# Both halves of a weight load split in one ACT and one DVE instruction, and the order of loads and block products that goes with it

## The chip, the cores and the metric

The kernel runs on one core of a Trainium2 chip. The metric is the device time of one execution in microseconds (us). Engines: PE multiplies matrices (PEld is its weight load), DVE, ACT and POOL work on vectors, SP issues most of the DMAs.

## The reference, cut to what matters

A two-layer encoder over 256 tokens of width 1024, in float32:

```python
for layer in range(DEPTH):                                   # DEPTH = 2
    h = h + _token_mixer(_rmsnorm(h, norm1[layer]), ...)
    h = h + _conv_ffn(_rmsnorm(h, norm2[layer]), ...)
return _rmsnorm(h, norm_f)

def _token_mixer(xn, w_in, w_pool, pool_scale, w_a, w_b, w_o, rel_bias):
    u, q, k, v, g_pool, g_attn = jnp.split(xn @ w_in, SPLITS, axis=-1)
    ...   # centred means of u; dilated attention of q, k, v with bias from rel_bias
    merged = jax.nn.sigmoid(g_pool) * (pool_out @ w_a) + jax.nn.sigmoid(g_attn) * (attn_out @ w_b)
    return merged @ w_o

def _conv_ffn(xn, w_up, conv_w, conv_b, w_down):             # d_ff = 2816
    a, gval = jnp.split(xn @ w_up, 2, axis=-1)
    a = conv of width 3 along the tokens, a channel at a time, + conv_b
    return (jax.nn.gelu(a) * gval) @ w_down
```

The weights (186 MB read from HBM) are used once each, so the kernel is a long stream: load a piece of weights, prepare it, multiply.

## The kernel before, in words

**Loads and splits.** Weights come in loads of 1 MB, `raw` in the profile (128 partitions x 4 x 512 floats; for `w_down` and `w_o` 2 x 1024). Three such buffers exist. PE multiplies in a reduced float32 form (fp32r), so each load is split in two halves of 128x1024, and each half in two terms: ACT makes `wh`, the rounded weights (a CAST, L259), and DVE makes `wl`, what the rounding lost (a subtraction, L261). There are five buffers of 128x1024 for `wh` and five for `wl`. PE then takes three products for each slice of weights: wh with x's high term, wl with it, wh with x's low term. These are the lines L798 (projections by tokens), L715, L716 and L717 (products into the residual: `w_down`, `w_o`) and L917 (block products). A 1 MB load gives 24 matmuls of 128x512.

**The class `Weights`** keeps the list of pieces (halves) in the order of their use. `_split` makes splits ahead of the products as buffers allow, and after each one calls `load(ahead(i))`, which issues loads on SP's queue. SP also issues the copies by which tensors change their layout through DRAM ("crossings": a write at L857, four reads into `zga`, `zg` and others at L864), and SP's queue runs in order. `run_between` runs steps of other work between the ACT and the DVE part of a split.

**The block.** One 2x2 block of `w_up`'s column groups in each layer's MLP (group `("w", 3)`), and one part of the projections in layer 1, are multiplied with seven products in place of eight. Each product has a name and two halves: 11, 22 and 21 take weights as loaded; T1 to T4 take sums of quadrants that DVE makes in place in a `raw` buffer (L344). 50 and 51 are the numbers of the two loads that hold these sums. In this text "T4" is the last product. The constant `BLOCK` gives the order; `"d"` stands for one piece (half a load) of `w_down`, multiplied at L715 to L717 in between. The products collect in four PSUM banks:

```python
BANK_OF = {"11": "p", "T1": "t", "22": "t", "T2": "q", "21": "p", "T3": "q", "T4": "q"}
```

T2, T3 and T4 add up in bank q. After T2 and again after T3 `add` reads bank q (a DVE sum into `kept`, L1692) and sends the result off (a DVE transpose, L852, and a crossing). So T4's matmuls can begin only when T3's `add` has read the bank. The MLP's own order is written by hand (`manual_schedule`, MLP_GROUPS, PAIR_PLACES); within a queue nothing overtakes. A half of 21, T1 to T4 or 11 is six matmuls, a "d" twelve.

**Norms.** Between the parts of a layer an RMSNorm turns the residual `h` (L607) into `xn` (L618), which PE transposes (L627); ACT and DVE make its two terms (L630, L631). During the MLP's first norm DVE also makes splits for the first groups.

**Attention bias.** `build_bias` makes the position bias of four heads and reads it from DRAM into `bt` with five DMAs (L559) once, in layer 0.

Of the kernel before, what the change touches and what calls it, by code (L numbers as in the profile page):

```python
# [52 lines left out]
    ("11", 0), ("11", 1), "d", ("T1", 0), ("T1", 1), "d", "d", ("22", 0), ("22", 1), "d", ("T2", 0), ("T2", 1), "d",  # L53
    ("21", 0), ("21", 1), "d", ("T3", 0), ("T3", 1), "d", "d", ("T4", 0), ("T4", 1),
# [64 lines left out]
class Weights:  # L119
# [6 lines left out]
    RAW, BUFS, LOOK = 3, 5, 3  # L126

    def __init__(self, tc, pool, idle, small):
# [7 lines left out]
        self.between = []  # L136
# [3 lines left out]
        self.sums = {}  # L140

    def add(self, src, shape, cuts, tag=None):

        n = len(self.loads)
        self.loads.append((src, shape, tag))
        return [(n, cut, c_shape) for cut, c_shape in cuts]

    def use(self, pieces, slots=()):
        slots = list(slots) + [None] * len(pieces)
        self.pieces += [p + (slot,) for p, slot in zip(pieces, slots)]  # L150

    def ahead(self, i):


        upto = min(n for n, *_ in self.pieces[i : i + 3])
# [52 lines left out]
    def _split(self, upto):  # L208
        nc = self.nc
        first = self.n_split  # L210
        while self.n_split < len(self.pieces):
            i = self.n_split
            n, cut, shape, slot = self.pieces[i]
            if i >= upto and (slot is None or i >= max(upto, first + 2) or i >= upto + 4 or i < 4):
                break
            if slot is None and len(self.live) == self.BUFS:
                break
            self.load(n + 1)
            with ExitStack() as queued:
                for insts, some in self.later:  # L220
                    for inst in insts if i in some else ():
# [10 lines left out]
    def run_between(self):  # L232

        while self.between:
            self.between.pop(0)()

    def open_next(self):
# [3 lines left out]
        n, cut, shape, slot = self.pieces[i]  # L241
        if slot is None:
            self.live.add(i)
            h, l = (
                self.pool.tile([P, *shape], F32R, tag=tag, bufs=self.BUFS, name=f"{tag}{i}")
                for tag in ("wh", "wl")
            )
# [44 lines left out]
    def free(self, i):  # L292
        self.live.discard(i)


@with_exitstack
def encoder(ctx, tc, x, w_in, w_pool, pool_scale, w_a, w_b, w_o, norm1, norm2, w_up, conv_w,
# [32 lines left out]
    def use_block(units, made, first):  # L330
# [9 lines left out]
        def sum_later(i, name, j):  # L340

            def make():
                one, other = terms[name]
                nc.vector.tensor_sub(out=raw(name, j), in0=raw(one, j), in1=raw(other, j))  # L344
# [3 lines left out]
        for j in range(2):  # L348
            sum_later(len(W.pieces) + first + j, "T1", j)
        behind = [u for u in units if len(u) > 2]  # L350
        for unit in units:
            if len(unit) > 2:
                W.use([unit])
                behind = behind[1:] or behind
                continue
            name, j = unit
            if name in SUMS:
                sum_later(len(W.pieces), SUMS[name], j)
            if name in ("22", "21"):
                W.use([made[name][j]])  # L360
            else:
                W.use([(behind[0][0], lambda t, name=name, j=j: raw(name, j), (2, 512))])
# [6 lines left out]
    def block(w, down, n, made):  # L369
# [3 lines left out]
        d += rows(down, 4 * P)  # L373
        made["21"] = quadrant(w, 1, DFF + n * 512)
        d += rows(down, 6 * P)
# [151 lines left out]
    bt = const.tile([P, HPG, NT * P], F32, name="bt")  # L527

    def build_bias():
# [25 lines left out]
        nc.sync.dma_start(out=fd[0].rearrange("(h e) -> h e", h=HPG), in_=fsb)  # L555
        yield
        for blk, kind in enumerate((4, 3, 1, 0, 2)):
            src = bass.AP(fd.tensor, fd.offset + kind * 256, [[1, P], [NT * 256, HPG], [1, P]])
            nc.sync.dma_start(out=bt[:, :, blk * P : (blk + 1) * P], in_=src)  # L559
        yield  # L560

    def bias_of(t, hh):

        b = bt[:, hh]
# [556 lines left out]
    for l in range(DEPTH):  # L1121
# [203 lines left out]
        if l == 0:  # L1325
            visits["u", 1, 0] = visits["u", 1, 2] = ((next, bias),)

# [439 lines left out]
```

## Time and profile before

| | before |
|---|---|
| three runs | 848.07, 847.58, 847.60 us; median 847.6 |
| profiled execution | 848.11 us, its span 846.3 us (1.8 us lie around it) |
| granted PE clock | 0.999 |
| busy | PE 838.7, PEld 699.3, DVE 665.5, ACT 531.1, POOL 35.5 us |
| moved by DMA | 214 MB, mean 253 GB/s |

Busy time of an engine that others wait for counts; busy time beside a busier engine does not. In the chain of waits each row is a piece of the work that ended last: its start, its length, the engine and the line. In the groups a row gives how often an instruction ran, its busy time and the mean of one. In the timeline the idle time before an instruction, and what ended it, stand in brackets. An instruction that starts while the one before it drains overlaps with it on paper: DVE instructions follow one another at some 0.08 us less than the length that is shown.

### The profile page before, as it was taken

What the parts mean: (1) busy time and instruction counts of PE and PEld (TensorE: products, weight loads), DVE (VectorE), ACT (ScalarE), POOL (GpSimd) and SP (SyncE); (2) the same over time, 40 slices, a digit from 0 to 9 for tenths busy, and PEclk for the clock granted to TensorE, in tenths of its full rate; (3) what the DMA queues carried; (4) which work ended last, traced back from release to release, by engine and by line L of the source; (5) the groups of instructions that cost most, each with busy time, mean ns of one, the idle gap of its engine ahead of it and who ended that gap; (6) DMA issues with size and microseconds to landing.
All of it is one profiled execution on the core that took longest, in us unless ns stands there. A gap on an engine that the chain in (4) does not pass through costs nothing.

```text
span 846.3 us, 10959 instructions
## 1 busy us (share of the span) xinstructions
PE 838.7 (99%) x3889; PEld 699.3 (83%) x3889; DVE 665.5 (79%) x860; ACT 531.1 (63%) x770; POOL 35.5 (4%) x96
## 2 busy tenths in 40 slices
PE   9999999999999999999999999999999999999997
PEld 7888888888888887888888888888888888888886
DVE  6968877757767799788898997868577867998884
ACT  7744556655554776488765555577455647757883
POOL 1720000000010000000000000000000100000000
PEclk9999999999999999999999999999999999999999
DMA  8699987796759886889857669968777499768861
GB/s 305 211 304 289 317 282 251 246 282 218 233 206 302 276 275 199 256 264 316 272 185 225 222 225 316 284 235 261 247 261 269 164 308 309 227 224 275 303 218 50
DMA packets 147967, 214.02 MB, mean 253 GB/s; under 512 B 7801, under 2 KB 69185, under 8 KB 147913
## 3 DMA queue, kind: packets, MB, share of 16 engines
q1 hardware_dynamic: 147480, 212.67, 76.8%
q10 hardware_dynamic: 432, 0.66, 0.2%
q8 instruction: 30, 0.49, 0.2%
q14 instruction: 25, 0.20, 0.1%
HBM read 186.02 MB, written 27.28 MB: 252 GB/s over the span
## 4 chain that ended last, share of the span: by engine, by line
PE 90%; DMA 3%; DVE 3%; ACT 2%; issue 1%; POOL 0%; ACTq 0%; SPq 0%; DVEq 0%; POOLq 0%
PE t_ps L798 54%; PE res_ps L716 6%; PE res_ps L715 6%; PE res_ps L717 6%; PE t_ps L917 4%; PE v_ps L798 3%; DMA raw<-in_w_up_dram 3%; PE v_ps L1101 3%; PE v_ps L917 2%; PE pool_ps L702 1%; PE v_ps L1000 1%; PE o_ps L1392 1%; PE s_ps L1344 1%; ACT wh L259 1%; DVE wl L261 1%; PE s_ps L1339 1%
## 5 line engine op out<-in xcount | busy, mean ns | idle before, releaser
L261 DVE TENSOR_TENSOR wl<-raw,wh 128x1024 fp32r<-128x1024 f32 x292 | 350.9, 1219 | 92.4 <-ACT wh L259 91.7
L798 PE MATMUL t_ps<-wh,x 128*128 128x512 f32 x1280 | 401.8, 390 | 0.0
L259 ACT CAST wh<-raw 128x1024 fp32r<-128x1024 f32 x292 | 302.1, 1048 | 158.8 <-PE t_ps L798 71.2
L798 PEld LDWEIGHTS t_ps<-wh,x 128*128 128x128 f32 x1280 | 240.3, 188 | 50.0
L798 PE MATMUL t_ps<-wl,x 128*128 128x512 f32 x640 | 249.0, 389 | 0.0
L798 PEld LDWEIGHTS t_ps<-wl,x 128*128 128x128 f32 x640 | 120.2, 188 | 24.7
L715 PE MATMUL res_ps<-wh,actq 128*128 128x512 f32 (+1 forms) x184 | 70.0, 380 | 0.0
L716 PE MATMUL res_ps<-wl,actq 128*128 128x512 f32 (+1 forms) x184 | 69.8, 380 | 0.0
L717 PE MATMUL res_ps<-wh,actk 128*128 128x512 f32 (+1 forms) x184 | 69.3, 380 | 0.0
L798 PE MATMUL t_ps<-wh,po 128*128 128x512 f32 x128 | 41.4, 395 | 0.0
L715 PEld LDWEIGHTS res_ps<-wh,actq 128*128 128x128 f32 x184 | 34.6, 188 | 6.7
L716 PEld LDWEIGHTS res_ps<-wl,actq 128*128 128x128 f32 x184 | 34.6, 188 | 6.7
L717 PEld LDWEIGHTS res_ps<-wh,actk 128*128 128x128 f32 x184 | 34.6, 188 | 6.5
L1604 ACT ACTIVATE a<-zga,prm 128x256 f32<-128x256 f32 x80 | 38.9, 512 | 0.0
L592 POOL TENSOR_SCALAR ss<-ss 128x1 f32<-128x1 f32 x8 | 3.1, 386 | 764.2 <-ACT junk L585 764.2
L344 DVE TENSOR_TENSOR raw<-raw,raw 128x1024 f32<-128x1024 f32 x24 | 29.3, 1222 | 0.0
L798 PEld LDWEIGHTS t_ps<-wh,po 128*128 128x128 f32 x128 | 24.0, 188 | 4.9
L715 PE MATMUL res_ps<-wh,m 128*128 128x512 f32 (+1 forms) x72 | 26.5, 368 | 0.0
L716 PE MATMUL res_ps<-wl,m 128*128 128x512 f32 (+1 forms) x72 | 26.3, 365 | 0.0
L717 PE MATMUL res_ps<-wh,m 128*128 128x512 f32 (+1 forms) x72 | 26.0, 365 | 0.0
L1608 DVE TENSOR_TENSOR y<-y,a 128x510 f32<-128x510 f32 x22 | 14.9, 679 | 13.6 <-ACT y L1602 13.6
L798 PE MATMUL t_ps<-wl,po 128*128 128x512 f32 x64 | 24.9, 390 | 0.0
(221 smaller groups left out, 1069.6 us busy)
## 6 DMA issues: line engine op xcount, KB each, us to landing
raw<-in_w_in_dram SPq DMA_DIRECT2D x58, 1024.0 KB
raw<-in_w_up_dram SPq DMA_DIRECT2D x40, 1024.0 KB
raw<-in_w_down_dram SPq DMA_DIRECT2D x22, 1024.0 KB
crossing<-crossing SPq DMA_DIRECT2D x22, 512.0 KB
crossing<-way SPq DMA_DIRECT2D x16, 512.0 KB
raw<-in_w_a_dram SPq DMA_DIRECT2D x8, 1024.0 KB
raw<-in_w_o_dram SPq DMA_DIRECT2D x8, 1024.0 KB
zga<-crossing SPq DMA_DIRECT2D x40, 128.0 KB
```

The source lines that it names most:

```text
L259: inst = nc.scalar.copy(out=h, in_=src)
L261: inst = self.rests[i] = nc.vector.tensor_sub(out=l, in0=src, in1=h.bitcast(F32))
L344: nc.vector.tensor_sub(out=raw(name, j), in0=raw(one, j), in1=raw(other, j))
L702: nc.tensor.matmul(out, w(k), x, start=(steps is first and k == 0), stop=(steps is last and k == nk - 1), skip_group_check=turns["rest"],)
L715: nc.tensor.matmul(ps, ah, wh, start=first, stop=False, skip_group_check=on)
L716: nc.tensor.matmul(ps, ah, wl, start=False, stop=False, skip_group_check=on)
L717: nc.tensor.matmul(ps, al, wh, start=False, stop=last, skip_group_check=on)
L798: nc.tensor.matmul(ps, x2[:, 2 * n + j, part, t, :], w[:, j, :], start=(n + m == 0), stop=(n == last and m == 5),)
L917: nc.tensor.matmul(ps, operands[name](part, 2 * j + c), w[:, c, :], start=(name in ("11", "T1") and j + m == 0), stop=(j == 1 and m == 5), ...
L1101: nc.tensor.matmul(ps[t], a[:, k, t, :], w[:, j, :], start=(k + m == 0), stop=(k == KD - 1 and m == 2),)
L1604: nc.scalar.mul(out=out, in_=a, mul=row(j, c))
L1608: nc.vector.tensor_add(out=y[:, :, 1:], in0=y[:, :, 1:], in1=t["a0"][:, :, : S - 1])
```

## The change

1. **Pairs.** Where `W.two` is set (the six projection groups with n other than 1 or of kind "u"; in the MLP all but the last two groups), both halves of a load are split by one ACT instruction and one DVE instruction of 128x2048 (L311 and L312 of the new kernel), once two neighbouring slots are free. The five `wh` and five `wl` buffers become six slots each. The sums for T1 to T4 are made over 128x2048 as well (L424).
2. **Loads.** There, `ahead` counts the `raw` buffers held, and issues the next load when one of three is given back.
3. **Orders.** `BLOCK` and `VALUES` put both halves of each unit together and change the places of the "d" pieces. Copies by ACT of the block's banks run before a split's ACT part (`at_once`) in place of after it.
4. **Bias.** `bt` holds two heads at a time. Five DMAs load the first two (SP's queue, in both layers), five more on ACT's queue the other two, in attention step 4.

```diff
 BLOCK = (
-    ("11", 0), ("11", 1), "d", ("T1", 0), ("T1", 1), "d", "d", ("22", 0), ("22", 1), "d", ("T2", 0), ("T2", 1), "d",
-    ("21", 0), ("21", 1), "d", ("T3", 0), ("T3", 1), "d", "d", ("T4", 0), ("T4", 1),
+    ("11", 0), ("11", 1), "d", "d", ("T1", 0), ("T1", 1), "d", "d", ("22", 0), ("22", 1), "d", "d",
+    ("T2", 0), ("T2", 1), "d", "d", ("T3", 0), ("T3", 1), ("21", 0), ("21", 1), ("T4", 0), ("T4", 1),
 )
...
-    RAW, BUFS, LOOK = 3, 5, 3
+    RAW, SLOTS, LOOK = 3, 6, 3
...
     def ahead(self, i):
+        if self.two:
+            upto = end = self.n_loaded
+            held = sum(
+                tag is None and self.last_use[n] > i
+                for n, (_, _, tag) in enumerate(self.loads[:upto]) if n > upto - 10
+            )
+            while held < self.RAW and end < len(self.loads) and self.not_before.get(end, i) <= i:
+                end += 1
+                if self.loads[end - 1][2] is None:
+                    held += 1
+                    upto = end
+            return upto
...
+            count = 1
+            if self.makes_two(i):
+                if self.two_slots() is not None:
+                    count = 2
+                elif i >= self.n_got + 2:
+                    break
...
-                for hi, lo, *_ in self.open_next():
+                for hi, lo, *_ in self.open_next(count):
+                    self.run_at_once()
                     hi()
                     self.run_between()
                     lo()
-                if i in self.sums:
-                    self.sums.pop(i)()
-            self.load(self.ahead(i))
+                for j in range(i, i + count):
+                    if j in self.sums:
+                        self.sums.pop(j)()
+            self.load(self.ahead(i + count - 1))
...
+                def both(n):
+                    if n == 0:
+                        return nc.scalar.copy(out=h, in_=src)
+                    inst = nc.vector.tensor_sub(out=l, in0=src, in1=h.bitcast(F32))
+                    self.rests[i] = self.rests[i + 1] = inst
+                    return inst
...
-    bt = const.tile([P, HPG, NT * P], F32, name="bt")
+    bt = const.tile([P, 2, NT * P], F32, name="bt")
...
-            4: ((W.bring_back,), (scores, 1)),
+            4: ((W.bring_back,), (scores, 1), (load_bias, 2, nc.scalar)),
...
             for kind, n in GROUPS:
+                W.two = n != 1 or kind == "u"
```

**Place 1: DVE at the end of layer 0's block.** The rows are splits (`wl<-raw,wh`), sums (`raw<-raw,raw`), `add` and its transpose. Before, raw_2535 holds T3, raw_2537 T4, raw_3004 the weights of 21, raw_2940 and raw_3006 pieces of `w_down`, raw_3087 the group after the block:

```order
290 L344 TENSOR_TENSOR raw_2537<-raw_3004,raw_2537 128x1024
291 L261 TENSOR_TENSOR wl_3060<-raw_3004,wh_3059 128x1024
292 L344 TENSOR_TENSOR raw_2537<-raw_3004,raw_2537 128x1024
293 L261 TENSOR_TENSOR wl_3071<-raw_2940,wh_3070 128x1024
294 L1692 TENSOR_TENSOR kept<-t_ps,kept 128x512
295 L852 STREAM_TRANSPOSE crossing<-kept 128x4x4x32
296 L261 TENSOR_TENSOR wl_3081<-raw_2535,wh_3080 128x1024
297 L261 TENSOR_TENSOR wl_3106<-raw_2535,wh_3105 128x1024
298 L261 TENSOR_TENSOR wl_3116<-raw_3006,wh_3115 128x1024
299 L261 TENSOR_TENSOR wl_3126<-raw_3006,wh_3125 128x1024
300 L261 TENSOR_TENSOR wl_3142<-raw_2537,wh_3141 128x1024
302 L1692 TENSOR_TENSOR kept<-t_ps,kept 128x512
```

Now raw_2311 holds T3, raw_2313 T2 and then T4, raw_2723 the weights of 21, raw_2690 two pieces of `w_down`, raw_2742 the group after the block:

```order
243 L312 TENSOR_TENSOR wl<-raw_2690,wh 128x2048
244 L312 TENSOR_TENSOR wl<-raw_2311,wh 128x2048
245 L1786 TENSOR_TENSOR kept<-t_ps,kept 128x512
246 L940 STREAM_TRANSPOSE crossing<-kept 128x4x4x32
247 L312 TENSOR_TENSOR wl<-raw_2723,wh 128x2048
248 L424 TENSOR_TENSOR raw_2313<-raw_2723,raw_2313 128x2048
249 L312 TENSOR_TENSOR wl<-raw_2313,wh 128x2048
250 L1786 TENSOR_TENSOR kept<-t_ps,kept 128x512
251 L940 STREAM_TRANSPOSE crossing<-kept 128x4x4x32
252 L312 TENSOR_TENSOR wl<-raw_2742,wh 128x2048
```

The sum that makes T4's weights stood ahead of T3's splits, with two pieces of `w_down` split after them; now it stands behind T3's and 21's splits, directly ahead of its own.

**Place 2: SP's queue at the start of layer 0's MLP.** Before (raw rows are 1 MB loads of `w_up`, crossing rows the write and zga and zg rows the four reads of a crossing):

```order
98 L178 DMA raw_2444<-in_w_up_dram 128x4x512
99 L857 DMA crossing<-crossing 128x2x512
100 L178 DMA raw_2537<-in_w_up_dram 128x4x512
101 L864 DMA zga<-crossing 32x8x128 x4
102 L178 DMA raw_2466<-in_w_up_dram 128x4x512
103 L178 DMA raw_2500<-in_w_up_dram 128x4x512
104 L857 DMA crossing<-crossing 128x2x512
105 L178 DMA raw_2539<-in_w_up_dram 128x4x512
106 L864 DMA zg<-crossing 32x8x128 x4
107 L178 DMA raw_2573<-in_w_up_dram 128x4x512
```

And now, where raw_2263, raw_2267, raw_2283, raw_2315, raw_2344 are the loads that raw_2444, raw_2466, raw_2500, raw_2539 and raw_2573 were, and raw_2313 is what raw_2537 was:

```order
98 L199 DMA raw_2263<-in_w_up_dram 128x4x512
99 L945 DMA crossing<-crossing 128x2x512
100 L199 DMA raw_2267<-in_w_up_dram 128x4x512
101 L952 DMA zga<-crossing 32x8x128 x4
102 L199 DMA raw_2283<-in_w_up_dram 128x4x512
103 L199 DMA raw_2313<-in_w_up_dram 128x4x512
104 L199 DMA raw_2315<-in_w_up_dram 128x4x512
105 L945 DMA crossing<-crossing 128x2x512
106 L199 DMA raw_2344<-in_w_up_dram 128x4x512
107 L952 DMA zg<-crossing 32x8x128 x4
```

The load that stood behind the four `zga` reads (raw_2466) now stands ahead of them, and so does raw_2573 ahead of the `zg` reads.

**Place 3: DVE in the norm ahead of layer 0's MLP.** Before (x_2207 is the second term of the transposed `xn`):

```order
216 L631 TENSOR_TENSOR x_2207<-xt_ps,x_2207 128x4x128
217 L261 TENSOR_TENSOR wl_2330<-raw_2137,wh_2329 128x1024
218 L618 SCALAR_TENSOR_TENSOR xn<-h,rstd,gain 128x256 x4
219 L631 TENSOR_TENSOR x_2207<-xt_ps,x_2207 128x4x128 x2
220 L852 STREAM_TRANSPOSE crossing<-v_ps 128x4x4x32
221 L261 TENSOR_TENSOR wl_2431<-raw_2218,wh_2430 128x1024
```

Now:

```order
189 L719 TENSOR_TENSOR x_2036<-xt_ps,x_2036 128x4x128
190 L335 TENSOR_TENSOR wl<-raw_1972,wh 128x1024
191 L335 TENSOR_TENSOR wl<-raw_2047,wh 128x1024
192 L706 SCALAR_TENSOR_TENSOR xn<-h,rstd,gain 128x256 x4
193 L719 TENSOR_TENSOR x_2036<-xt_ps,x_2036 128x4x128 x2
194 L940 STREAM_TRANSPOSE crossing<-v_ps 128x4x4x32
```

One more split of 128x1024 stands ahead of the second token half's four `xn`.

More of the change, by code (lines that the diff above doesn't have):

```diff
@@ L140, in __init__ @@
         self.sums = {}
+        self.slots = [pool.tile([P, self.SLOTS, 1024], F32R, tag=tag, name=tag) for tag in ("wh", "wl")]
+        self.freed = {slot: slot - self.SLOTS for slot in range(self.SLOTS)}
+        self.slot_of, self.n_freed = {}, 0
     def add(self, src, shape, cuts, tag=None):
@@ L338, in raw, with whole, sum_later @@
             return W.raw[made[name][0][0]][:, 2 * j : 2 * j + 2]
-        def sum_later(i, name, j):
+        def whole(name):
+            return W.raw[made[name][0][0]]
+        def sum_later(i, name):
             def make():
                 one, other = terms[name]
-                nc.vector.tensor_sub(out=raw(name, j), in0=raw(one, j), in1=raw(other, j))
+                nc.vector.tensor_sub(out=whole(name), in0=whole(one), in1=whole(other))
             W.sums[i] = make
-        for j in range(2):
-            sum_later(len(W.pieces) + first + j, "T1", j)
-        behind = [u for u in units if len(u) > 2]
+        sum_later(len(W.pieces) + first + 1, "T1")
         for unit in units:
@@ L361, in use_block @@
             else:
-                W.use([(behind[0][0], lambda t, name=name, j=j: raw(name, j), (2, 512))])
+                W.use([(
+                    made[name][0][0], lambda t, name=name, j=j: raw(name, j), (2, 512),
+                    False if j else lambda t, name=name: whole(name),
+                )])
     def first_quadrants(w, n):
@@ L1640, in at_place @@
         def at_place(p, make, *first):
+            W.at_once = [step for step in first if step in by_scalar]
+            first = [step for step in first if step not in by_scalar]
             W.between = [*first, *(step for _, _, step in sorted(between.pop(p, ()), key=lambda x: x[:2]))]
@@ L1708, in encoder @@
             for kind, n in MLP_GROUPS[1:]:
+                W.two = (kind, n) not in MLP_GROUPS[-2:]
                 ps = None
```

93 lines of the change are left out of this document (69 added, 24 removed), and 10 rows, old and new, of the table VALUES.

## The prediction

> **What bounds the kernel now.** I read the engines' busy time first, then the windows by stage (columns: length, then busy us and count of PE, PEld, DVE, ACT and POOL, the granted clock, the DMA share, GB/s), then the chain of waits where PE was not full.
>
> ```profile
> span 846.3 us, 10959 instructions
> PE 838.7 (99%) x3889; PEld 699.3 (83%) x3889; DVE 665.5 (79%) x860; ACT 531.1 (63%) x770; POOL 35.5 (4%) x96
> ```
> ```profile
> 0.00:20.00 20.00, 19.15 (x87) 15.77 (x88) 12.25 (x21) 13.66 (x26) 3.89 (x12) 1.00 0.91 321
> 20.00:240.00 220.00, 220.00 (x1035) 184.16 (x1034) 164.32 (x234) 124.58 (x174) 19.79 (x59) 1.00 0.82 267
> ...
> 300.00:320.00 20.00, 19.59 (x87) 15.81 (x86) 18.28 (x23) 16.66 (x27) 0.00 (x0) 1.00 0.78 239
> 320.00:340.00 20.00, 20.00 (x90) 16.57 (x89) 19.97 (x19) 12.54 (x14) 0.00 (x0) 1.00 0.64 210
> ...
> 420.00:440.00 20.00, 19.69 (x104) 16.19 (x103) 17.44 (x28) 12.73 (x24) 3.34 (x7) 1.00 0.70 236
> 440.00:650.00 210.00, 210.00 (x989) 176.07 (x988) 167.10 (x221) 123.86 (x165) 0.00 (x0) 1.00 0.76 245
> ```
>
> PE is the bound almost everywhere: through 220 us and again through 210 us it is never idle, although DVE and ACT work there at 75 to 80% and 57 to 59%. Making DVE and ACT cheaper is therefore worth nothing by itself. Idle PE is seen at 300 to 320 (0.41 us) and 420 to 440 (0.31 us). In 320 to 340 DVE is full (19.97 of 20) while PE still keeps going: the block lives on the distance that its splits have.
>
> The chain of waits shows PE's pace and the two stalls:
>
> ```profile
> 317.26 0.64 DVE crossing L852
> 318.03 3.03 PE t_ps L917 x12
> ...
> 337.38 2.72 PE t_ps L917 x12
> ...
> 350.98 2.72 PE t_ps L917 x12
> 353.70 32.64 PE t_ps L798 x144
> ...
> 422.87 0.50 DVE xn L618
> ...
> 429.56 0.50 DVE xn L618
> 430.10 0.83 PE xt_ps L627 x4
> ...
> 432.33 0.44 PE xt_ps L627 x4
> ```
>
> Twelve matmuls take 2.72 us and 144 take 32.64: 0.2267 us each both times, so the pace does not change with the work around it. At 318 a dozen took 3.03, 0.31 too long, which with the idle 0.41 makes a stall of 0.72. At 430 four transposes took 0.83 against 0.44, 0.39 too long, with the idle 0.31 together 0.70. No more than about 1.4 us of stalls can be won after the start, 0.17%. What a run can tell from no change is 0.2%, 1.7 us (845.9 or less; 849.3 or more).
>
> **The change, part by part.** PE does the same matmuls, so the sum is the stalls that go against the stalls that come.
>
> *Price of a pair.* No 128x2048 instruction was run. From the groups:
>
> ```profile
> L261 DVE TENSOR_TENSOR wl<-raw,wh 128x1024 fp32r<-128x1024 f32 x292 | 350.9, 1219 | 92.4 <-ACT wh L259 91.7
> L259 ACT CAST wh<-raw 128x1024 fp32r<-128x1024 f32 x292 | 302.1, 1048 | 158.8 <-PE t_ps L798 71.2 <-DMA raw<-in_w_up_dram 40.4 <-PE res_ps L717 23.5
> L1625 DVE TENSOR_TENSOR actk<-g,actq 128x512 fp32r<-128x512 f32 x22 | 15.1, 686 | 0.0
> L1624 ACT CAST actq<-g 128x512 fp32r<-128x512 f32 x22 | 13.6, 619 | 8.8 <-DVE g L1616 8.8
> ```
>
> DVE: 1219 + 2 x (1219 - 686) = 2285 ns, ACT: 1048 + 2 x (1048 - 619) = 1906 ns. Upper ends are two halves, 2.44 and 2.10. In place of two halves that saves some 0.15 and 0.19 us, on engines that do not bound. I take 2.29 and 1.91. [...]
>
> *The stall at 317 goes.* It began with a late load. SP's queue (before, place 2) held a load behind the four `zga` reads:
>
> ```profile
> 265.21 1.81 SPq L864 DMA_DIRECT2D zga<-crossing  x4
> 267.13 0.94 SPq L178 DMA_DIRECT2D raw<-in_w_up_dram  x2
> ```
> ```profile
> ACT wh L259 <- DMA raw<-in_w_up_dram: 40.4, 15, 7.5
> ```
>
> The load went out at 267.13; ACT waited up to 7.5 us for such loads, DVE fell behind and was full up to the transpose at 317.26. Now this load stands ahead of the reads and is issued when a buffer is given back, and DVE has some 0.1 us less for each pair. I take the whole 0.72 away (other end: 0, if DVE is late all the same).
>
> *The norms.* Ahead of the MLP (place 3) one more split stands ahead of the second `xn` group:
>
> ```profile
> 247.35 1.22 DVE L261 TENSOR_TENSOR wl<-raw,wh 128x1024 fp32r<-128x1024 f32 x1
> 249.02 1.67 DVE L618 SCALAR_TENSOR_TENSOR xn<-h,rstd,gain 128x256 f32<-128x256 f32 x4 [0.46 <-POOL rstd L597]
> ```
> ```profile
> 249.89 0.60 PE L627 MATMUL xt_ps<-ident,xn 128*128 128x128 f32 x4
> ```
>
> DVE was free at 248.48 (247.35 + 1.13) and waited for POOL; a further split ends that pitch at 249.61, 0.6 later than 249.02. PE's transposes started 0.05 after two `xn` were there (249.02 + 2 x 0.41). PE now does one matmul of 0.23 ahead of them, so 0.6 - 0.05 - 0.23 = 0.3 us is new idle time, in each layer: +0.6 (ends 0 and 1.2). In the norm between the layers, PE's order puts two matmuls (0.45) ahead of the second transposes, but one more split stands there too; of the 0.70 I take half away, -0.35 (ends 0 and -0.70).
>
> *The end of the block.* This is the largest term. T4's weights are now a sum that needs 21's split, which stands behind T3's split, and `add` of T3 stands behind T4's split (place 1). The block and what follows end where they did, so on PE's clock of before T2 runs from 337.38, two pieces of `w_down` from 340.10, T3 from 345.54, 21 from 348.26, T4 from 350.98, five by 2.72 us after 337.38. There are three pairs of slots: T3's split can begin only when the pieces ahead of T2 are multiplied, at 337.38. The rows for the steps:
>
> ```profile
> 324.05 1.22 DVE L261 TENSOR_TENSOR wl<-raw,wh 128x1024 fp32r<-128x1024 f32 x1
> 325.19 1.22 DVE L344 TENSOR_TENSOR raw<-raw,raw 128x1024 f32<-128x1024 f32 x1
> ...
> 338.80 0.69 DVE L1692 TENSOR_TENSOR kept<-t_ps,kept 128x512 f32<-128x512 f32 x1
> 339.53 0.71 DVE L852 STREAM_TRANSPOSE crossing<-kept 128x512 f32<-128x512 f32 x1
> 340.17 6.86 DVE L261 TENSOR_TENSOR wl<-raw,wh 128x1024 fp32r<-128x1024 f32 x6
> ```
> ```profile
> 337.42 1.06 ACT L259 CAST wh<-raw 128x1024 fp32r<-128x1024 f32 x1 [1.37 <-PE res_ps L717]
> ```
>
> A cast starts 0.04 after PE's release (337.42). Then: T3's cast to 339.33; T3's subtraction 339.40 to 341.69 (the next can start 0.08 before that); `add` of T2 at 341.61 (to the next 0.73); its transpose at 342.34 (0.64); 21's subtraction at 342.98 (2.20 to the next); the sum for T4 at 345.18 to 347.47, a subtraction priced as a split, as the two kinds are equal in the rows (1.22); T4's cast 347.50 to 349.41; T4's subtraction 349.48 to 351.77; `add` of T3 351.69 to 352.38. T4 starts at 352.45 against 350.98: a stall of 1.5 us. Before, the sums for T4 stood ahead of the `add` at 338.80 and T4's splits in the run of six at 340.17, so nothing waited. Layer 1 has the same order on both engines:
>
> ```profile
> 733.81 2.87 PE t_ps L917 x12
> ...
> 753.03 2.72 PE t_ps L917 x12
> ...
> 766.63 2.72 PE t_ps L917 x12
> ```
>
> The last two lie where 337.38 and 350.98 lie in layer 0, 415.65 later, so again 1.5: together +3.0. Ends: +4.0 if a pair costs two halves (five steps by some 0.1 more each) and the group after it is late too; +1.6 if T3's split has a slot 0.7 earlier than I read. The next group's split (raw_2742) ends about 2.2 us after `add`, at 354.6, ahead of its use at 355.2.
>
> *Elsewhere nothing.* The sums among layer 1's projections have 8 to 11 us between a slot's release and its use, one of 5.4 against a need of 4.4 (a cast, a split and their waits). (A release is a slot's last matmul; between it and the use lie 36 to 48 matmuls, once 24.) Five bias DMAs on ACT's queue stand behind the second scores' `p`, and the third scores' sums need them:
>
> ```profile
> 0.72 0.39 ACTq L475 DMA_DIRECT2D h<-in_x_dram  x1
> ```
> ```profile
> 154.33 1.32 ACT L1368 ACTIVATE p<-p,rz 128x512 f32<-128x512 f32 x2
> ```
> ```profile
> 160.64 0.68 DVE L1351 CUSTOM_DVE_ANT_0 s<-s_ps,bt 128x512 f32<-128x512 f32 x1
> ```
>
> 5 x 0.39 = 2.0 us of issue from 155.6 on; the casts behind them start 2 us later, on an ACT that is idle 41% of 440 to 650, and the last bias goes out at 157.6, 3 us before its use. Should it land late, DVE waits 1 to 2 us with its splits behind it; at 75 to 80% busy it catches up. I take 0; without that cover it would be 2 us in each layer. Start and end keep their order.
>
> **Sum.** -0.72 - 0.35 + 0.6 + 3.0 = +2.5 us. The profiled execution took 848.11 (span 846.3 and 1.8 around it), giving 850.6; it stands 0.5 above the median of the three, 847.6, so the forecast is 850.1.
>
> **The rivals.**
>
> *A, the block's end is covered: not slower.* The one mechanism is T4's chain: 13.6 us of PE from 337.38 to 350.98 against 15.1 of chain. It carries four DVE pairs and two casts. It decides at 1.5 us: if the pairs took 1.91 in place of 2.29, or T3's split began at 335.9, no stall would come. The slope of 512 to 1024 speaks against the first, the three slot pairs against the second. It would give 847.6 - 0.72 - 0.35 + 0.6 = 847.1; with half of the stall left, 848.6: both within 0.2%.
>
> *B, more of the block is late.* DVE was full at 320 to 340, and a pair's split is usable only when all of it is done, 1.1 us later than the first half was. If the first products (11, T1, 22) also meet late pairs, the stall of 317 stays (+0.7) and comes in layer 1 too (there its dozen took 2.87, 0.15 long already), and T4's end is +4.0: 847.6 + 4.0 + 0.7 + 0.6 - 0.35 = 852.6. For it speaks the full DVE, against it that loads come earlier.
>
> [...]
>
> **How the numbers follow.** Forecast (849.3 to 851.5): 0.46. A: 0.32, of which within 0.2% nearly all. B (851.5 to 853): 0.14. C: 0.08, half of it below 845.9. Slower: 0.46 + 0.14 = 0.60; faster: 0.04; within 0.2%: 0.36. The range reaches from A's low part, 846.8, to B, 852.2; outside it lie half of B and most of C. If it is slower, 849.3 to 852.
>
> **What would show it.** Right: after about 350 and 766 us PE idles 1 to 2 us ahead of a block product (L1005), released by DVE's `add` (L1786); that row stands in the waits and DVE's splits (L312) at 2.2 to 2.3 us; PE is full at 310 to 320; 0.3 idle at about 250 and 666. Wrong: PE full through both blocks' ends, L312 well under 2.2 us, or T4's cast (L311) starting at or before 346. PE idle among the projections would mean that loads or slots, which I price at nothing, run short.

## The result, and the profile after

The changed kernel takes 856.77 us (median of four runs, 854.14 to 857.12) against 847.82 (847.58 to 848.07) for the kernel before: ratio 1.0099 [1.0078, 1.0119], 9 us slower. The profiled execution is the one of 857.12.

The head of the page after, with ACT's DMA queue (q10) and, in the last three rows, the groups of the pairs (L312, L311) and of the sums (L424):

```profile
span 855.3 us, 10716 instructions
PE 841.8 (98%) x3889; PEld 699.9 (82%) x3889; DVE 657.3 (77%) x753; ACT 516.3 (60%) x675; POOL 33.8 (4%) x96
...
q10 hardware_dynamic: 3152, 1.97, 0.9%
...
L312 DVE TENSOR_TENSOR wl<-raw,wh 128x2048 fp32r<-128x2048 f32 x95 | 216.9, 2285 | 54.6 <-ACT wh L311 54.5
...
L311 ACT CAST wh<-raw 128x2048 fp32r<-128x2048 f32 x95 | 181.0, 1909 | 91.7 <-PE t_ps L886 46.7
...
L424 DVE TENSOR_TENSOR raw<-raw,raw 128x2048 f32<-128x2048 f32 x12 | 27.4, 2284 | 0.0
```

The pairs cost what was estimated (2285 ns, 1909 ns). The bias DMAs on ACT's queue show in q10, where the kernel before had 432 packets. DVE has 8.2 us less to do and ACT 14.8, and the kernel is 9 us longer. PE's waits after (line, what it waited for, us in total, times, longest) and its windows (columns as above):

```profile
PE t_ps L1005 <- DVE kept L1786: 3.1, 2, 1.5
PE xt_ps L715 <- DVE xn L706: 1.4, 2, 1.1
...
PE t_ps L886 <- DVE way L940: 0.4, 1, 0.4
PE o_ps L1478 <- DVE ptl L1469: 0.3, 1, 0.3
PE v_ps L886 <- DVE x L719: 0.3, 1, 0.3
```
```profile
0.00:20.00 20.00, 18.54 (x81) 15.36 (x82) 10.70 (x19) 12.05 (x24) 2.87 (x11) 1.00 0.90 321
...
240.00:260.00 20.00, 19.67 (x106) 16.37 (x105) 14.62 (x25) 13.10 (x23) 3.06 (x7) 1.00 0.48 164
300.00:320.00 20.00, 20.00 (x90) 16.56 (x89) 16.42 (x17) 13.91 (x20) 0.00 (x0) 1.00 0.77 258
...
340.00:360.00 20.00, 18.46 (x82) 15.00 (x81) 16.41 (x11) 11.05 (x6) 0.00 (x0) 1.00 0.43 136
420.00:440.00 20.00, 18.92 (x102) 15.68 (x100) 16.19 (x24) 13.26 (x23) 3.95 (x7) 1.00 0.88 313
580.00:620.00 40.00, 39.42 (x213) 33.62 (x213) 28.46 (x42) 24.09 (x37) 0.00 (x0) 1.00 0.87 269
```

300 to 320 is full, which it was not before; 340 to 360 has lost 1.5 us, and the wait at L1005 stands twice, once in each layer. The other losses are small and spread over places most of which the prediction had priced at nothing.

To add them up I took, from the trace, the start-to-start time of each matmul beyond its pace (0.227 us at 512 columns, 0.118 at 256, 0.111 at 128). The sum over the kernel is 8.9 us more after than before; the two spans differ by 9.0, so nothing large is missing. The rows below hold 8.4 of it; the rest lies in pieces of less than 0.2 us. Of the changed kernel there are three more profiled executions (the runs e5, e13 and e14 below), of the kernel before one more (e15):

| us lost on PE | before, two profiles | after, first | after, the other three |
|---|---|---|---|
| first 41 us | 3.4, 3.6 | 4.9 | 3.6, 4.3, 5.2 |
| layout copies near 135 | 0, 0 | 0.7 | 0, 0, 0 |
| attention, layer 0 and 1 | 0, 0 | 0.3 + 1.1 | 1.6, 1.1, 0.9 |
| norm ahead of the MLP, layer 0 and 1 | 0, 0 | 0.6 + 0.1 | 0.6, 1.5, 1.2 |
| near 317 | 0.65, 0 | 0 | 0, 0, 0 |
| T4, both layers | 0, 0 | 1.7 + 1.7 | 3.4, 3.4, 3.4 |
| between the layers | 0.75, 0.75 | 2.1 | 1.7, 1.7, 2.0 |

**T4.** DVE, then T3's cast on ACT and T4's first matmul on PE, at the end of the block after (timeline):

```profile
342.16 2.29 DVE L312 TENSOR_TENSOR wl<-raw,wh 128x2048 fp32r<-128x2048 f32 x1 [1.47 <-ACT wh L311]
344.37 0.68 DVE L1786 TENSOR_TENSOR kept<-t_ps,kept 128x512 f32<-128x512 f32 x1
...
345.72 2.25 DVE L312 TENSOR_TENSOR wl<-raw,wh 128x2048 fp32r<-128x2048 f32 x1
347.89 2.28 DVE L424 TENSOR_TENSOR raw<-raw,raw 128x2048 f32<-128x2048 f32 x1
352.23 2.29 DVE L312 TENSOR_TENSOR wl<-raw,wh 128x2048 fp32r<-128x2048 f32 x1 [2.05 <-ACT wh L311]
354.44 0.68 DVE L1786 TENSOR_TENSOR kept<-t_ps,kept 128x512 f32<-128x512 f32 x1
```
```profile
340.21 1.91 ACT L311 CAST wh<-raw 128x2048 fp32r<-128x2048 f32 x1 [3.08 <-PE res_ps L805]
```
```profile
355.27 0.47 PE L1005 MATMUL t_ps<-wh,x 128*128 128x512 f32 x1 [1.54 <-DVE kept L1786]
```

This is the predicted chain, step by step: T3's split, `add` of T2, 21's split, the sum, T4's split, `add` of T3. PE's matmul ahead of it began at 353.34, so T4 was due at 353.57; it began at 355.27, 1.70 later.

**Attention.** SP's queue after, and the chain that ended in the stall:

```profile
572.33 0.46 SPq L199 DMA_DIRECT2D raw<-in_w_a_dram  x1
576.05 5.54 SPq L952 DMA_DIRECT2D turned_p<-turning  x4
```
```profile
572.33 8.45 DMA raw<-in_w_a_dram
...
580.79 0.30 SPq L952
...
581.14 3.58 DMA turned_p<-turning
...
585.47 0.70 DVE ptl L1469
...
586.22 0.86 PE o_ps L1478 x5
```

Four small reads took 5.54 us to issue, because the queue stood in the midst of them until a 1 MB load that has nothing to do with them had landed (572.33 + 8.45 = 580.78). The trace's DMA records name the semaphore (a counter) that each DMA raises and those that it waits for: the 462 DMAs of SP and ACT before take eight of them (100 and 103 to 109) in rotation. Before, the load had number 104 and the four reads behind it 105 to 108. After, the load has 106, the first two reads 107 and 100, and the five bias DMAs 108, 109, 103, 104 and 105, so the third read gets 106 as well. Its record names a wait for 106, and it began at 580.79, 0.01 behind the landing of the load. e2 and e4 below try this.

**The norms.** The chain after between the layers, in both its stalls:

```profile
419.52 4.97 DMA raw<-in_w_in_dram
...
424.57 0.69 ACT wh L333
...
425.53 1.04 ACT wh L333
426.57 0.63 ACT junk L673 x2
...
428.22 0.50 DVE xn L706
...
430.76 4.99 DMA raw<-in_w_in_dram
...
435.78 1.92 ACT wh L311
...
440.01 0.61 DVE x L719
```

On ACT two casts that wait for a load (at 424.57 and 425.53) run ahead of the norm's square sums (`junk`, at 426.57), which take 0.63 us and which everything waits for; then a pair's cast, which waits for the next load (at 435.78), and its split run ahead of x's second term (at 440.01). Ahead of layer 0's MLP the chain reads the same, with one cast that waits:

```profile
234.70 8.54 DMA raw<-in_w_up_dram
...
243.34 1.05 ACT wh L333
244.39 0.63 ACT junk L673 x2
```

### The profile page after: what moved, and what is told of

It reads as the page before. It is cut to its first block, busy times and chain, and to the rows that moved or that the text cites. A ratio compares the mean times of both kernels' runs of the same rounds, so it can differ in the third digit from the quotient of the medians.

```text
span 855.3 us, 10716 instructions
## 1 busy us (share of the span) xinstructions
PE 841.8 (98%) x3889; PEld 699.9 (82%) x3889; DVE 657.3 (77%) x753; ACT 516.3 (60%) x675; POOL 33.8 (4%) x96
## 4 chain that ended last, share of the span: by engine, by line
PE 73%; DMA 9%; DVE 8%; ACT 5%; issue 3%; SPq 1%; POOL 0%; ACTq 0%; DVEq 0%; POOLq 0%
PE t_ps L886 45%; PE res_ps L804 4%; PE res_ps L803 4%; PE res_ps L805 4%; PE t_ps L1005 3%; PE v_ps L886 3%; DVE wl L312 3%; PE v_ps L1189 3%; PE v_ps L1005 2%; DMA raw<-in_w_in_dram 2%; ACT wh L311 2%; PE v_ps L1088 1%; DVE wl L335 1%; DMA crossing<-way 1%; DMA raw<-in_w_up_dram 1%
## 5 line engine op out<-in xcount | busy, mean ns | idle before, releaser
L312 DVE TENSOR_TENSOR wl<-raw,wh 128x2048 fp32r<-128x2048 f32 x95 | 216.9, 2285 | 54.6 <-ACT wh L311 54.5
L311 ACT CAST wh<-raw 128x2048 fp32r<-128x2048 f32 x95 | 181.0, 1909 | 91.7 <-PE t_ps L886 46.7
L335 DVE TENSOR_TENSOR wl<-raw,wh 128x1024 fp32r<-128x1024 f32 x102 | 121.3, 1217 | 36.1 <-ACT wh L333 36.1
L333 ACT CAST wh<-raw 128x1024 fp32r<-128x1024 f32 x102 | 104.6, 1048 | 26.9 <-PE t_ps L886 14.9
L940 DVE STREAM_TRANSPOSE crossing<-t_ps 128x512 f32<-128x512 f32 x36 | 23.7, 693 | 6.8 <-DMA crossing<-crossing 6.4
L424 DVE TENSOR_TENSOR raw<-raw,raw 128x2048 f32<-128x2048 f32 x12 | 27.4, 2284 | 0.0
L1704 ACT ACTIVATE y<-y 128x512 f32<-128x512 f32 x22 | 13.9, 631 | 20.9 <-DVE y L1701 20.9
L803 PE MATMUL res_ps<-wh,m 128*128 128x512 f32 (+1 forms) x72 | 26.5, 367 | 0.0
```

The source lines that it names most:

```text
L311: return nc.scalar.copy(out=h, in_=src)
L312: inst = nc.vector.tensor_sub(out=l, in0=src, in1=h.bitcast(F32))
L333: inst = nc.scalar.copy(out=h, in_=src)
L335: inst = self.rests[i] = nc.vector.tensor_sub(out=l, in0=src, in1=h.bitcast(F32))
L424: nc.vector.tensor_sub(out=whole(name), in0=whole(one), in1=whole(other))
L803: nc.tensor.matmul(ps, ah, wh, start=first, stop=False, skip_group_check=on)
```

## The experiments

The theory: the 9 us are several stalls of separate causes, T4's chain (3.4), the bias DMAs (1 to 1.5), and splits and casts ahead of the norms' small steps (2 to 3); the pairs themselves cost nothing. The rival: they have one cause, the pairs with their load rule.

**e1: 21 ahead of T3, so that no long chain ends at T4.** 21's load is moved ahead of the last `w_down` load as well.

```diff
-    ("T2", 0), ("T2", 1), "d", "d", ("T3", 0), ("T3", 1), ("21", 0), ("21", 1), ("T4", 0), ("T4", 1),
+    ("T2", 0), ("T2", 1), ("21", 0), ("21", 1), ("T3", 0), ("T3", 1), "d", "d", ("T4", 0), ("T4", 1),
```

> The changed kernel, with one move in its block: 21 is multiplied ahead of T3, and two pieces of w_down lie between T3 and T4 (as many as before the change). Theory: the stall ahead of T4 is the chain 21's split, T4's sum, T4's split, add; with 5.4 us of other products ahead of T4 it goes in both layers, 2 x 1.7 us: 856.8 - 3.5 = 853.3, and no wait of a block product for add is left. Rival: with pairs the block as a whole is short of DVE, so that the stall moves to another product of it: 856 or more.

851.51 us, 1.0047 [1.0032, 1.0062]. The stalls ahead of T4 are gone, and 0.44 us ahead of T3 came in each layer, again a wait for `add`, which the expectation had excluded. T4's order was the largest single part of the loss. The time lies 1.8 us below the expectation; e1's profile shows neither the late start (3.5 us) nor the stall at 135, which T4's order does not explain.

**e2: the other two heads' bias on POOL's queue.**

```diff
-            4: ((W.bring_back,), (scores, 1), (load_bias, 2, nc.scalar)),
+            4: ((W.bring_back,), (scores, 1), (load_bias, 2, nc.gpsimd)),
```

> The changed kernel, with the five DMAs for the second two heads' bias on POOL's queue in place of ACT's. Theory: on ACT's queue these DMAs take part in the waits of SP's DMAs (one of the four reads of turned p is held until an unrelated 1 MB load has landed), which makes the stalls at 165 (0.33 us) and 585 (1.1 us); on POOL's queue both go: 856.8 - 1.4 = 855.4. Rival: the reads are late because the loads come earlier and fill the DMA engines; then the stalls stay: 856.8.

854.54 us, 1.0085 [1.0068, 1.0102]. SP's reads in e2, and PE in the stage that held the stall:

```profile
573.47 1.81 SPq L952 DMA_DIRECT2D turned_p<-turning  x4
```
```profile
580.00:620.00 40.00, 40.00 (x212) 34.25 (x211) 26.11 (x40) 22.30 (x35) 0.00 (x0) 1.00 0.88 293
```

The reads are issued in 1.81 us again and PE is full: with the five DMAs off ACT's queue, and nothing else changed, the stalls of attention are gone.

**e3: both edits, e1 and e2.**

> Both of the moves of the other two runs at once. Theory: they add up, 856.8 - 3.5 - 1.4 = 851.9; what is left over before (4 us) lies at the start, at 135 and between the layers. Rival (block short of DVE, bias innocent): 856 or more.

850.64 us, 1.0038 [1.0023, 1.0053], beside 847.42 for the kernel before on the same chip: 0.9 below e1 and 3.9 below e2. Each edit gains beside the other too, though less than alone against 856.77 (3.9 beside 5.3, and 0.9 beside 2.2), which was measured apart from these three, with more of the stalls that come and go; 3.2 us stay, of which its profile shows 0.9 in the two T3 stalls, 1.3 between the layers and 0.7 at 243.

**e4: the kernel before with the bias in two parts alone** (five DMAs on SP's queue, five on ACT's, as in the change).

```diff
-    bt = const.tile([P, HPG, NT * P], F32, name="bt")
+    bt = const.tile([P, 2, NT * P], F32, name="bt")
...
-            4: ((W.bring_back,), (scores, 1)),
+            4: ((W.bring_back,), (scores, 1), (load_bias, 2, nc.scalar)),
```

> The kernel before, with the bias in two parts alone (two heads in bt, the first two loaded by SP in each layer, the other two by ACT's queue in attention step 4). Theory: the same reads are held in the same way, some 0.3 and 1.1 us at about 163 and 577: 847.7 + 1.4 = 849.1. Rival (the loads' order makes those stalls): 847.7, no change.

849.0 us, 1.002 [1.001, 1.0029], with stalls of 0.5 at 163 and 0.7 at 580. The reads behind the second (SP's queue in e4) took 4.78 us to issue, against 1.82 in the kernel before:

```profile
571.28 4.78 SPq L873 DMA_DIRECT2D turned_p<-turning  x4
```

The bias is thus a cost of its own, with or without pairs.

**e5, e13, e14: the changed kernel again, e15: the kernel before again,** unchanged, to see which stalls belong to the kernel and which to one execution.

> The changed kernel once more, unaltered, for more executions. Theory: the stalls at the block's end (3.4 us), in the attention (1.4), in the norms (0.6 and, between the layers, 1.4 more than before) are in every execution and, less 0.7 for the stall at 317 that went, make 847.4 + 6.1 = 853.5; the 1.5 us in the first 20 us and the 0.7 at 135 are in some executions only, so times spread from 853.5 to 857. Rival: these two are in each execution too, and the median stays at 856.8 with a profile that shows both again.

> The changed kernel, for a third profile. Theory: the stalls of 1.7 ahead of T4, 0.4 and 1.1 in the attention and 0.8 or more at 424 are there again to 0.1 us, since program order makes them; the late start (4.9 against 3.4 us of PE idle in the first 41 us) and the 0.7 at 135 come and go. Rival: they are there in each execution above 856.

> The changed kernel, for a fourth profile, with the same expectation as for the third: fixed stalls ahead of T4 and in the attention, a start and a copy at 135 that come and go.

> The kernel before, unaltered, for a second profile. Theory: its slower executions (849 to 850 among 847.3 to 847.6) are the late start as well, 1.3 to 1.8 us, which then is no part of the change's loss; a profile at 847.5 shows 3.4 us there, one at 849 shows 5. Rival: its start is 3.4 us at any time.

857.86 (854.56 to 858.62), 855.77, 855.76 and 848.25 us (847.43 to 849.98); their profiles are the last columns of the table above. T4's stalls are there each time to 0.02 us; those of attention, of the norms and between the layers always, in changing sizes; the stall at 135 once in four. So e13's expectation, sizes equal to 0.1 us, held for T4 alone, and e5's median lies above the 857 that it allowed. e13 also lost 0.8 us at 837, in the last products, which no other profile of the changed kernel shows. The start is 3.6 to 5.2, before 3.4 and 3.6. And the stall at 317, from which the prediction took its first gain, is missing in the second profile of the kernel before: it comes and goes.

**e6: pairs and the new load rule in the MLP alone.**

```diff
-                W.two = n != 1 or kind == "u"
+                W.two = False
```

> The changed kernel with pairs (and the loads' new rule) in the MLP alone, none in the projection groups. Theory: pairs in the first projection group hold up the terms of x behind a cast of 1.9 us (0.9 us of stalls at 437 to 441), and nothing else comes of them in the projections: 856.8 - 0.9 = 855.9. Rival: the pairs and the early loads of the projections are also what makes the attention's reads and the layout copy at 135 late: 854 or less.

859.99 us, 1.0145 [1.0122, 1.0168]. A miss: 2 us slower than e5 on the same chip, not faster. The stalls of x's second term (438) are gone, but 1.1 and 1.5 came at 416 and 427 and some 4 us between 516 and 545, among layer 1's projections. The orders around the pairs need the pairs or the load rule there.

**e7: e3, and no more than five halves live outside the pairs,** so that the sixth slot opens no split ahead of the norms.

```diff
-            if slot is None and not self.freed:
+            if slot is None and (not self.freed or not self.two and len(self.live) > 4):
```

> The kernel with 21 moved and the bias loads on POOL's queue (850.6), and outside of pairs no more than five halves split at a time, as before the change. Theory: it was the sixth slot that let one more split go ahead of xn in each norm; with five, DVE's order there is the old one, and the stall at 243 (0.73) and half of that at 424 (0.36) go: 850.6 - 0.9 = 849.7. Rival: the norms are late because the loads and splits ahead of them are; then the stalls stay: 850.6.

852.11 us, 1.0043 [1.0027, 1.0059]; e5 on the same chip took 857.86. PE ahead of layer 0's MLP in e7:

```profile
240.00:260.00 20.00, 20.00 (x109) 17.14 (x108) 15.86 (x26) 11.62 (x20) 3.06 (x6) 1.00 0.45 150
```

The stall at 243 is gone, and e8 and e12, which have the same limit, do not show it either, so there the sixth slot was the cause. Between the layers it was not: 1.0 at 434 to 437 stayed, and the stall at 424, 0.4 in e3, became 1.9 (1.0 in e8, 2.2 in e12). The time is no better than e3's.

**e8: e7 with another order of the block (11, T1, two pieces, 22, ...) and the first group by halves.**

```diff
-    ("11", 0), ("11", 1), "d", "d", ("T1", 0), ("T1", 1), "d", "d", ("22", 0), ("22", 1), "d", "d",
-    ("T2", 0), ("T2", 1), "d", "d", ("T3", 0), ("T3", 1), ("21", 0), ("21", 1), ("T4", 0), ("T4", 1),
+    ("11", 0), ("11", 1), ("T1", 0), ("T1", 1), "d", "d", ("22", 0), ("22", 1), "d", "d", ("T2", 0), ("T2", 1),
+    "d", "d", ("21", 0), ("21", 1), ("T3", 0), ("T3", 1), "d", "d", ("T4", 0), ("T4", 1),
```

> As the run with five live halves, with pairs in the first projection group taken away too, and a block in the order 11, T1, two pieces of w_down, 22, two, T2, two, 21, T3, two, T4. Theory: each unit then has two units of 8 us between the release of its slot and its use, so the 0.44 us ahead of T3 in each layer goes, and so do 0.9 us between the layers: 849.7 - 1.8 = 847.9, and with the stall at 317 gone at best 847.0, no more than the kernel before. Rival: 11 and T1 one behind the other make DVE late at the block's start, 849 or more.

857.9 us, 1.0109 [1.0084, 1.0135]. T1 now came too early: it waits 2.4 us in each layer for DVE's transpose, and PE then takes 0.427 us a matmul in place of 0.227 for some 3 us (last section).

**e9: e3 without pairs (every split by halves), with the orders and the load rule kept.**

```diff
-        if not self.two or i < self.n_scaled or i + 1 >= len(self.pieces):
+        if True or i < self.n_scaled or i + 1 >= len(self.pieces):
```

> The kernel with 21 moved and the bias loads on POOL's queue (1.0038 of before), with every split made by halves; the loads' rule, the orders and the six slots stay. Theory: pairs buy nothing that PE waits for, and a pair's cast of 1.9 us in the first projection group holds x's terms up for 0.9 us: without pairs 850.6 - 0.9 = 849.7, ratio 1.0027. Rival: the block and the projections of layer 1 need the 0.1 to 0.2 us that each pair saves DVE and ACT; without it new stalls come there, 852 or more.

857.69 us, 1.0119 [1.0099, 1.014], 7 us above e3's 850.64 (on another chip). The stall ahead of T3 is gone, but PE waits 4.5 us for `xn` in two norms: between the layers two casts that wait for PE to free their slots stand ahead of `junk` on ACT. The rival's time came, but not its place: the blocks and the projections of layer 1 (440 to 570) show no stall of 0.2 us, and the losses lie ahead of the norms and, 1.7 more than in e3, in the start.

**e10: e3 with pairs and the old load rule.**

```diff
-        if self.two:
+        if False:
             upto = end = self.n_loaded
```

> The kernel with 21 moved and the bias loads on POOL's queue (1.0038 of before), with the old rule for when loads are issued; pairs and orders stay. Theory: it is the new rule that puts a load ahead of the layout copy's reads at the start of the MLP and takes the 0.7 us at 317 away; with the old one that stall is back: 851.3, ratio 1.0046. Rival: the stall went since DVE had less to do with pairs, and the new rule fills the DMA engines ahead of copies: without it 849.5 or less.

889.21 us, 1.0497 [1.0476, 1.0518]. Both theories expected far too little: a pair's cast needs the whole load (in the first profile after, the one at 435.78 began 0.03 behind the landing), and with the old rule the pairs come too late (PE waits 7.0 us for `wl` and 6.3 for `wh` in the products into the residual alone). Pairs and load rule belong together: the rule without pairs (e9) and the pairs without the rule (e10) are both worse than the two of them.

**e11 and e16: e3 with the first group behind the norm by halves,** so that no pair's cast stands ahead of x's terms.

```diff
-                W.two = n != 1 or kind == "u"
+                W.two = n != 1
```

> The kernel with 21 moved and the bias loads on POOL's queue (1.0038 of before), with the first projection group split by halves. Theory: the stalls at 433 to 437 (0.9 us) are x's terms behind a pair's cast that itself waits for its load; by halves they go, in layer 1 alone: 849.7, ratio 1.0027. Rival: x's terms wait for the load whatever the cast's size: no change, 850.6.

> The kernel with 21 moved, the bias loads on POOL's queue and the first projection group by halves, for a second profile. Theory: no stall of x's terms at 434 to 437, as in the first profile; the stall at 424 hangs on the landing of one load and is anywhere from 0.2 to 1.3 us. Rival: halves in the first group took both away, and 424 shows 0.2 again.

853.21 (1.0057 [1.0043, 1.0072]) and 851.35 us (1.0037 [1.0021, 1.0053]). PE at 430 to 440 in e3, then in e11:

```profile
430.00:440.00 10.00, 9.57 (x45) 7.24 (x44) 8.88 (x12) 6.14 (x7) 0.00 (x0) 1.00 0.61 226
```
```profile
430.00:440.00 10.00, 10.00 (x48) 7.97 (x47) 9.76 (x13) 6.50 (x10) 0.08 (x1) 1.00 0.66 248
```

The second stall between the layers goes, which shows its cause: the pair's cast and split ahead of x's terms. The stall ahead of layer 0's MLP is 1.0 in both profiles (0.7 in e3), and the time is no better than e3's. e11's profiled execution, 850.18, is the fastest of its six; what the others lost is not seen.

**e12: e7, the first group by halves, and no pairs for the MLP's pieces of `w_down`.**

```diff
-                W.two = (kind, n) not in MLP_GROUPS[-2:]
+                W.two = kind != "d"
```

> As the run with the first group by halves, and besides no more than five halves at a time outside of pairs, and no pairs in the MLP's last four groups, where only w_down is multiplied: around each norm the splits are those of the kernel before. Theory: what is lost between the layers is what stands ahead of the norm's sums of squares and xn on ACT and DVE; with the old order there the norms cost what they did (0.3 at 243, 0.7 at 424 to 430): 849.7 - 0.4 - 0.6 = 848.7, ratio 1.0015, the rest being 0.9 ahead of T3 in the two blocks. Rival: the stall between the layers comes from the loads, which stay late: 849.7.

853.25 us, 1.0066 [1.0045, 1.0087]. The stall at 243 is gone again, but 2.2 stand at 424, 0.4 came at 280 and at 322, and those ahead of T3 stayed, with 0.4 and 0.7. None of the variants came below the kernel before; e3 and e16 are the nearest, 0.4% above it.

## Why the prediction was right or wrong

Its sum was +2.5 us; the first profile after stands +9.0 above that of before. Term by term:

| term | forecast | first profile after | |
|---|---|---|---|
| stall at 317 goes | -0.72 | -0.65 | right here, but no sure gain (e15) |
| T4's chain | +3.0 | +3.4 | right, 0.2 small in each layer |
| norms ahead of the MLP | +0.6 | +0.7 | right size, wrong chain |
| norm between the layers | -0.35 | +1.35 | wrong sign |
| bias ("I take 0") | 0 | +1.4 | wrong |
| "Start and end keep their order" | 0 | +1.5 | wrong or chance: open |
| copies of layer 0 near 135 | 0 | +0.7 | once in four |

Of the 6.5 us between the forecast and this profile the norm between the layers makes 1.7, the bias 1.4 and T4 0.4; the start and the copies, 2.2 together, come and go.

The right part is the largest: the chain, its place, the releaser and both layers. Of T4's 0.2 the trace shows where: T2 began 13.6 us ahead of T4's due time, at 339.97, and T3's cast 0.24 later (340.21), where the prediction took 0.04 from a cast of before. Rivals A and C fell with that. For C, with its 0.08, half of it below 845.9, the profile after has this: one subtraction of 128x2048 took 2285 ns against 2 x 1219 for two of 128x1024, but of the 8.2 us less that DVE was busy, PE got at most 0.65. Rival B's mechanism (T1 and 22 late) did not come either, though the time went beyond its 852.6.

**One step that failed** is "Elsewhere nothing" on the bias. It counted what the DMAs cost on the queue on which they are issued (2.0 us on ACT) and when the last lands. What they did was on another queue: SP's reads of the second scores waited for a load. The prediction's own "without that cover it would be 2 us in each layer" stood for a late landing, which is not what happened. The five also took 3.5 and 2.9 us to issue on ACT (156.93 to 160.40, 576.70 to 579.56), not 2.0. e2 and e4 show the cause from both sides; the size is 0.9 to 1.6 us in the four profiles of the changed kernel and 1.2 in e4.

**The other**, and the larger, is the norm between the layers. The prediction weighed one more split on DVE against two matmuls and took half of the stall away. It looked at DVE, where the norm's steps had stood before, and not at ACT's queue, where one more cast now stands ahead of `junk`; the rows of before for that place, in ACT's timeline, are

```profile
419.41 1.05 ACT L259 CAST wh<-raw 128x1024 fp32r<-128x1024 f32 x1 [0.28 <-DMA raw<-in_w_in_dram]
421.12 0.63 ACT L585 ACTIVATE junk<-h 128x512 f32<-128x512 f32 x1 [0.65 <-DVE h L607]
```

There `junk` waited for h, its own input, and for no cast. After, it waits for two casts that wait for a load, and the load is late because DVE gave its buffer back late (418.32 + 1.15 is the split ahead of its issue at 419.52). The norm ahead of the MLP failed in the same way, with the right number by chance: the forecast put 0.3 at the second `xn` in each layer; the stall came at the first, in layer 0 mostly, and through ACT. e7, e8 and e12 (243) and e11 and e16 (434 to 437) show two of these causes. That of the first stall between the layers (424) is read from the chain alone. It is 0.6 to 1.5 us in the six profiles with the bias on ACT's queue and pairs (the changed kernel, e1, e6), 0.2 to 0.5 in e2, e3, e11 and e16, with the bias on POOL's (0.4 in the kernel before and in e4), and larger again with the limit of five halves. So the bias may have a part in it; by which path no run shows.

**What stays open.** Executions of the changed kernel spread over 4.5 us (854.1 to 858.6), those of before over 3 (847.2 to 850.3). Of the changed kernel's executions above 857.12 us none was profiled. Part of the spread is the start, 3.6 to 5.2 us after, where the profiles name late first loads (of x in the first profile, of the weights in e13). In e14 PE waits for no load: its pace is slow. Six of its first products, from 6.91 to 9.47, take 0.427 us each in place of 0.227, 1.2 us lost, and full clock is on record from 10.04 on; in the first profile it is from 8.68 on, in both of the kernel before, e5 and e13 from 4.45 to 5.70. Only two starts of before were profiled, so whether the late start belongs to the change is not settled; nor is why the norms' stalls change from 0.6 to 1.5.

## What to carry to other kernels

Fewer and larger instructions on engines that do not bound gave nothing here and moved the time at which a buffer comes free or a small step gets its turn: price such a change by what stands behind the longer instruction on each queue, above all the 0.6 us steps that a norm waits for. The DMAs that were added to ACT's queue stalled SP's through a shared semaphore (5.54 us of issue, 1.81 in e2), so look at the issue times of all queues, not at the new transfers. A load rule, its slots and the size of a split are one design: either half alone cost 7 and 39 us more than both (e9, e10 against e3).

## What the runs showed of the hardware

Two things. First, PE's pace falls after some stalls, and not at once. PE in e8 by windows (the granted clock is the third number from the end), rows of its timeline behind the stall, and two windows of e9 around its stall:

```profile
316.60:320.01 3.41, 1.03 (x5) 0.89 (x6) 2.73 (x5) 3.14 (x4) 0.00 (x0) 1.00 0.00 0
320.01:323.42 3.41, 3.41 (x10) 2.67 (x9) 3.39 (x2) 1.59 (x1) 0.00 (x0) 0.50 0.66 178
323.43:326.84 3.41, 3.41 (x17) 2.81 (x16) 3.41 (x3) 2.41 (x2) 0.00 (x0) 1.00 1.01 367
```
```profile
319.29 0.40 PE L1006 MATMUL t_ps<-wl,sx 128*128 128x512 f32 x1
319.52 0.62 PE L1006 MATMUL t_ps<-wh,sx 128*128 128x512 f32 x2
...
321.22 0.63 PE L1006 MATMUL t_ps<-wl,sx 128*128 128x512 f32 x1
...
322.50 0.63 PE L1006 MATMUL t_ps<-wl,sx 128*128 128x512 f32 x1
```
```profile
426.36:429.77 3.41, 2.02 (x15) 1.73 (x13) 1.68 (x3) 2.77 (x5) 0.01 (x1) 1.00 0.97 324
429.77:433.18 3.41, 2.00 (x17) 2.01 (x18) 2.46 (x6) 1.48 (x5) 1.27 (x3) 1.00 0.52 195
```

After 2.4 us of idle the first matmuls follow one another at 319.52 - 319.29 = 0.23 us; later three take 322.50 - 321.22 = 1.28, 0.427 each, until about 323. Seven such matmuls cost 0.2 each, some 1.4 us on top of the stall. The same came after layer 1's stall at 736 and in e10, where the granted clock was 0.57 from 534 to 538. T4's 1.7 us were not followed by it, and e9's 2.96 us at 428 neither.

The clock records of the traces show when. In the two first profiles the record of full clock runs from 5.70 to 845.38 (before) and from 8.68 to 851.77 (after), 839.68 and 843.09 us: 246 and 247 steps of 3.413. In e8 the clock is 0.50 from 320.01 to 323.43 and from 739.85 to 743.26, a step each, and 122 steps lie between the two. Counted from the start of the span, the edges lie elsewhere in each of the three. The step ahead of e8's first slow one left PE idle for 2.38 us (by its busy time in the profile), and in the first profile after, the last step ahead of 851.77, behind which the clock is 0.50, left 2.65. None of these was followed by a step below full clock: the one from 838.55 in the first profile before, with 1.74 us idle; those with T4's stalls, with 1.54 and 1.53; and the two with 1.39 and 1.41 into which an edge at 429.77 cut e9's stall.

Second, four small reads were held in the midst of their issue, in the changed kernel's first profile until a 1 MB load had landed that shares a semaphore with the third: 5.54 us there, 4.78 in e4 and 3.67 in e1, against 1.8 in the kernel before and in e2, followed by PE stalls of 1.1, 0.7 and 0.5 us.
